# Retention's values as one block product of seven, and the second retention beside its output product, in a two-layer hybrid decoder

## The chip, the cores and the metric

The kernel runs on one core of a Trainium2 chip. The metric is the device time of one execution in microseconds (us); the time of a version is the median of several runs. All products use fp32 data that is split into a high and a low part in the fp32r format, so that three matmuls make one product of full precision.

## The reference, cut to what matters

The program is a decoder trunk of two layers over 512 tokens and a model width of 1024. Each layer computes, from the normalised input h:

```
z   = h @ W_in            # attn q,k,v | ret q,k,v,g | gate_a | gate_b
A   = sliding-window attention(q, k, v) with rotary q/k and sinks
B   = retention(ret q, ret k, ret v), normed per head, * silu(ret g)
y   = sigmoid(gate_a) * (A @ W_a) + sigmoid(gate_b) * (B @ W_b)
x   = x + y @ W_out
x   = x + relu(RMSNorm(x) @ W_up)^2 @ W_down
```

Retention has 4 heads with keys of 128 and values of 256 columns. Its values are the product of the normalised input (512 x 1024) with a 1024 x 1024 part of W_in. That product is what the change computes in another way.

## The kernel before, in words

**Data.** Activations lie transposed in SBUF: a tile `xh`/`xl` of 8 k-tiles of 128 features x 512 tokens (high and low part of the input times the norm's gain). The norm's factor per token is applied where a product is evacuated from PSUM. `products` (L350 to L357) issues three matmuls for each pair of operands: high by high (L355), low of one by high of the other (L356, L357). There are two pools of PSUM banks of 128 x 512: `ps_mm` with five and `ps_aux` with three.

**Weights.** All weights come in units of 128 x 1024 (512 KB). `unit_order` (from L56) lists them in the order in which TensorE uses them. SyncE loads a unit into one of five `raw` buffers (L192), four units ahead (`AHEAD`); ACT makes its high part (`hi<-raw`, L308), VectorE the low part (`lo<-raw,hi`, L309), three units ahead (`SPLIT`), into four buffers each. The load of a unit waits until the buffer's last unit has been split.

**Sums of weights.** The MLP's products already use a block scheme with seven block products in place of eight. It needs sums of weight blocks, which GpSimd makes in DRAM: `sum_steps` (L205 to L234) yields steps of one copy and one accumulate (DMA with an addition), each 512 KB or 1 MB. `pace` (L238 to L246) is called behind many evacuations; at every second call a one-column copy on GpSimd (`mark`) waits for that evacuation, and then the next step's DMAs are issued. A copy is accumulated on one step later, and the accumulate waits for it.

**Order of a layer's first half.** The q/k/v group and the chunks of q; then eight chunks of gate_a, with the attention as `background`: a generator, of which `advance` runs one piece at certain points of the chunks, and `drain` the rest. Then `qk(0)` (retention's key and query of head 0), four chunks of retention's gate (`rg0` to `rg3`), `drain`, `qk(1)`, `load_decay(0)`, `values(0)`, the product with w_a, `qk(2)` and `qk(3)` with `retention(0)` as background, `values(1)`, `drain`, `retention(1)` as background beside `rg4` to `rg7` and four chunks of gate_b, `drain`, the product with w_b, w_out, and the MLP. The scheduler of the framework puts each engine's instructions in its final order. The engines run their own lists in order and meet at semaphores.

**The lines of this case.**

- `values(pair)` (L826 to L845): for two heads, 4 units of weights. The input blocks are the stationary operand; the weights move. Four banks, one for each block of 128 tokens, 96 matmuls of 128 x 512. Evacuation by ACT (L378) and VectorE (L379) with the norm's factor as a column scale.
- `weighted(n)` (L722 to L725): the attention's output of a block of 128 tokens: two banks `pv`, per bank a copy on ACT (`whole<-pv`, L724) and an addition on VectorE (L725), then `split` (L375, L376), which writes `a_h` and `a_l`; in the profile these rows are `r<-whole`. They are the input of the product with w_a.
- `rotate` (L594 to L601): two half copies on ACT (`rot<-mm`, L595, L596) and three operations on VectorE, for each key and query.
- `silu(i)` (L865, L866): the sigmoid of retention's gate (`sig<-z`) and its product.
- `load_decay` (L941 to L943): loads the decay matrices of two heads into a buffer of `big` (`dm`), 512 KB.
- the product with w_a: four units, eight chunks of 12 matmuls. Each ends with `mixed[c] = mixed[c] * ps` on VectorE (L1001, `x<-x,mm`) and a `pace`.
- `beside` and `put_k`/`put_q`: rotated q and k, then copies of 64 KB inside SBUF on SyncE's queue (`r<-qlo`, `r<-r`), which place the two heads of a group beside each other for the scores.
- `Head` (L880 on): `scores` (`ret`, with the decay applied by VectorE at L895), `outputs` (`r`), `norm`, `finish`, which writes `ret[2h]` and `ret[2h+1]`, the input of w_b.
- `group` (L414 on): a product of four banks over four units, with an optional call between units.

`big` has six buffers of 128 x 1024 in turn, for tables, decay, `z`, sums and the like.

Of the kernel before, what the change touches and what calls it, by code (L numbers as in the profile page):

```python
# [40 lines left out]
O_GA = O_RG + RET_HEADS * RET_V  # L41
O_GB = O_GA + D

N_IN = 46
N_BLOCK = 8
N_PAIR = 14
UNIT = 1024
# [8 lines left out]
def unit_order(layer):  # L56

    order = [("w_in", i) for i in range(4 + 2 + 8 + 2 + 4 + 2)]
    order += [("w_in", i) for i in range(22, 26)]
    order += [("w_a", i) for i in range(4)]  # L60
    order += [("w_in", i) for i in range(26, 42)]
    order += [("w_b", i) for i in range(4)]
    order += [("w_in", i) for i in range(42, 46)]
# [48 lines left out]


@with_exitstack
def decoder(ctx, tc, xT, x_first, w_in, w_a, w_b, w_out, w_up, w_pair, w_down, w_end, tables, decay, band, g_last, out):
    nc = tc.nc
    weights = {"w_in": w_in, "w_a": w_a, "w_b": w_b, "w_out": w_out, "w_up": w_up, "w_down": w_down}

# [60 lines left out]
    def load_until(n):  # L179
        while state["loaded"] < min(n, len(order)):  # L180
            i = state["loaded"]
            layer, name, j = order[i][:3]
            if name == "pair":
                load_part(i)
            elif name == "block":
                load_block(i)
            else:
                raws[i] = raw_tile()
                for at in halves(i):
                    queue = nc.scalar if i == 0 and at.start == 0 else nc.sync  # L190
                    source = w_end[j] if name == "w_end" else weights[name][layer, j]
                    queue.dma_start(raws[i][:, at], source[:, at])  # L192
                    if i < 3:
                        load_x()
            state["loaded"] += 1
# [6 lines left out]
    sums_up = [dram.tile([N_PAIR, P, UNIT], F32, name=f"sums_up{l}") for l in range(DEPTH)]  # L202
    sums_down = [dram.tile([N_BLOCK, P, 2 * UNIT], F32, name=f"sums_down{l}") for l in range(DEPTH)]
    sums_last = dram.tile([P, 2, UNIT], F32, name="sums_last")

    def sum_steps(layer):

        whole = N_BLOCK if layer < DEPTH - 1 else N_BLOCK - 1
        jobs = []
        for e in range(N_BLOCK):  # L210
            if e:
                jobs += [(sums_up[layer][n], w_pair[layer, n], UNIT) for n in (2 * e - 2, 2 * e - 1)]
            if e < whole:
                jobs.append((sums_down[layer][e], w_down[layer, e], 2 * UNIT))
        last = None
        for job in jobs + [None]:
            if job:
                to, source, n = job
                nc.gpsimd.dma_start(to, source[:, :n])
            if last:  # L220
                to, source, n = last
                nc.gpsimd.dma_start(to, source[:, n // 2 : n // 2 + n], accum_op=ALU.add)
# [63 lines left out]
    def add_block(i):  # L286
        e, part = order[i][2:]
        if part in (2, 4) and e < N_BLOCK - 1:
            raws[i] = raws.pop(i - 2)
            nc.vector.tensor_tensor(raws[i], raws[i], raws.pop(i - 1), ALU.add)  # L290

    def split_until(n):
        while state["split"] < min(n, len(order)):
            i = state["split"]
            load_until(i + AHEAD)
            name, part = order[i][1], order[i][-1]
            if name == "pair":
                add_part(i)
            elif name == "block":
# [4 lines left out]
            for at in (LEFT,) if name == "pair" and part == 3 else halves(i):  # L304
# [2 lines left out]
                else:  # L307
                    nc.scalar.activation(hi[:, at], raw[:, at], AF.Copy)  # L308
                nc.vector.tensor_tensor(lo[:, at], raw[:, at], f32(hi[:, at]), ALU.subtract)  # L309
            if not (name == "pair" and part < 2 or name == "block" and part < 4 and order[i][2] < N_BLOCK - 1):  # L310
                raws.pop(i)
            parts[i] = (hi, lo)
            state["split"] += 1
# [101 lines left out]
    def group(name, layer, moving, evacuates, meanwhile=None, low_last=None):  # L415
# [3 lines left out]
        for u in range(4):  # L419
# [6 lines left out]
            if low_last:  # L426
# [151 lines left out]
    def layer_body(layer):  # L578
# [48 lines left out]

        def put_k(ps):
            r = rotate(ps, attn_tabs, layer == 0)
            lo = big("klo")[:, 0, :]  # L630
            for g in range(N_KV):
                nc.scalar.activation(kh[g], r, AF.Copy)
# [27 lines left out]
        def put_q(c):  # L660
            def put(ps):
                r = rotate(ps, attn_tabs, layer == 0 and c < 2)
                if c % 2 == 0:
                    qlo[:] = [big("qlo")]
                lo = qlo[0][:, c % 2, :]
# [158 lines left out]

        rv = {}

        def values(pair):

            banks = [bank(ps_mm, "rv") for _ in range(NB)]
            for u in range(4):  # L830
                hi, lo = unit("w_in", layer)
                for j in range(2):
                    k = 2 * u + j
                    cols = slice(j * T, (j + 1) * T)
                    for b, ps in enumerate(banks):
                        at = slice(b * P, (b + 1) * P)
                        products(
                            ps, [((xh[:, k, at], xl[:, k, at]), (hi[:, cols], lo[:, cols]))], k == 0, k == KD - 1
                        )
                    advance()  # L840
            for b, ps in enumerate(banks):
                hi, lo = slots.one(), slots.one()
                split(view(hi), view(lo), ps, rms_mix.columns[:, b : b + 1])
                rv[pair, b] = (hi, lo)
                pace(f32(view(hi)))  # L845

        rg, rg_next = {}, {}

# [142 lines left out]
        for u in range(4):  # L991
            hi, lo = unit("w_a", layer)
            for j in range(2):
# [5 lines left out]
                    pairs.append(((hi[:, cols], lo[:, cols]), aT[k]))  # L999
                products(ps, pairs, True, True)  # L1000
                nc.vector.tensor_tensor(mixed[c], mixed[c], ps, ALU.mult)  # L1001
                pace(mixed[c])
# [12 lines left out]

# [13 lines left out]
        def put_mixed(c):  # L1029
            def put(ps):  # L1030
                m = temp("m")
                nc.vector.tensor_tensor(m, ps, gates[c], ALU.mult)
                nc.vector.tensor_tensor(m, m, mixed[c], ALU.add)
                hi, lo = slots.one(), slots.one()
                split(view(hi), view(lo), m)
                ms[c] = (hi, lo)

            return put

        rT = [tuple(view(s) for s in ret[k]) for k in range(KD)]  # L1040
        group("w_b", layer, rT, [put_mixed(c) for c in range(4)])
        for c in range(4, KD):
            gate_tile(c)
            chunk("w_in", layer, xs, gate(gates[c]))
# [3 lines left out]
            slots.give(*ret.pop(k))  # L1048


        source = xT if layer == 0 else spill
        for c in range(KD):
            nc.sync.dma_start(x[:, c, :], source[:, c, :])

        def put_x(c):
            def put(ps):
                nc.vector.tensor_tensor(x[:, c, :], x[:, c, :], ps, ALU.add)
                scaled_input(c, g_mlp)
                squared_input(c, g_mlp)

            return put
# [452 lines left out]
def _w_in_units(w):  # L1514
# [17 lines left out]
    units += qk(0)  # L1532
    units += _units_chunks(w, O_RG + r(T))
    units += qk(1)
    units += _units_group(w, O_RV + r(T))
    units += qk(2) + qk(3)
    units += _units_group(w, O_RV + T + r(T))
    units += _units_chunks(w, O_RG + T + r(T))
    units += _units_chunks(w, O_GB + r(D))
    return units  # L1540
# [2 lines left out]
def _pairs(w):  # L1543
# [2 lines left out]
    return [  # L1546
        np.concatenate([a[:, :H], b[:, :H], b[:, H:], a[:, H:]], 1) for a, b in zip(units[::2], units[1::2])
    ]


def _down_blocks(w):
# [42 lines left out]
def _laid_out(x, g_mix, w_in, sinks, w_a, w_b, w_out, g_mlp, w_up, w_down, g_final):  # L1594
# [9 lines left out]
        "xT": xT,  # L1604
        "x_first": np.concatenate([sinks, gains, xT[:, 0, :]], 1),
        "w_in": _stack(w_in, _w_in_units),
        "w_a": _stack(w_a, lambda w: _units_chunks(w[wa_rows], r(D))),
        "w_b": _stack(w_b, _half_grouped),
        "w_out": _stack(w_out, _half_grouped),
# [27 lines left out]
```

## Time and profile before

| | us |
|---|---|
| median of 3 runs | 1478.72 |
| runs | 1478.6, 1478.72, 1480.43 |
| the profiled execution's own time | 1480.34 |
| its span in the profile | 1478.6 |
| TensorE busy | 1467.4 |
| VectorE busy | 1079.6 |
| ACT busy | 914.0 |
| GpSimd busy | 195.3 |

The profile is of one execution. Its own time is 1.7 us above its span, and 1.6 above the median of the runs. PE is TensorE, DVE is VectorE, SP is SyncE (its queue of DMA issues is SPq). A row of a timeline has the start, the duration, the engine, the line, the operation, and output and input by the program's names; in brackets stands the idle time before it and what ended it. A matmul's duration in the profile is modelled and overlaps the next one's: the spacing of starts is what a matmul costs. A row of the DMA view has the number of issues, the size of each and the median time from issue to landing.

### The profile page before, as it was taken

The numbers are of one execution on the slowest core, as the hardware profiler recorded it, in microseconds if no ns is written. First come the engines' busy times: TensorE is split into PE (matmuls) and PEld (weight loads), VectorE is DVE, ScalarE is ACT, GpSimd is POOL, SyncE is SP. The second block draws the span as 40 slices with busy tenths as digits, with TensorE's granted clock in tenths as the row PEclk, the third lists the DMA queues.
The fourth block names the chain that finished last, engine by engine and source line by source line (L and its number), as shares of the span: only waits on it lengthen the run. The fifth ranks groups of instructions, "written<-read, shape, count | busy, mean of one in ns | idle before, by whom it ended". The sixth has DMA issues, their size and how long they took to land.

```text
span 1478.6 us, 21314 instructions
## 1 busy us (share of the span) xinstructions
PE 1467.4 (99%) x7799; PEld 1266.5 (86%) x7799; DVE 1079.6 (73%) x1639; ACT 914.0 (62%) x1501; POOL 195.3 (13%) x282
## 2 busy tenths in 40 slices
PE   9999999999999999999999999999999999999998
PEld 7888888888889999999888888888888899999997
DVE  6878568664577888888778686686546778888885
ACT  6656445533467777777756573555325777777775
POOL 0101121001001111112201012111000111111120
PEclk9999999999999999999999999999999999999999
DMA  7663996767315677666956539976432377777664
GB/s 259 174 191 82 310 271 162 197 184 214 118 65 192 188 197 190 167 184 183 302 172 207 157 101 309 267 190 184 146 128 89 114 202 195 189 197 186 174 191 148
DMA packets 92984, 272.61 MB, mean 184 GB/s; under 512 B 10832, under 2 KB 10960, under 8 KB 89040
## 3 DMA queue, kind: packets, MB, share of 16 engines
q1 hardware_dynamic: 60816, 169.27, 32.9%
q0 software_dynamic: 31344, 100.68, 30.9%
q8 instruction: 61, 1.00, 0.3%
q10 hardware_dynamic: 720, 1.31, 0.2%
q14 instruction: 43, 0.35, 0.1%
HBM read 231.37 MB, written 99.09 MB: 223 GB/s over the span
## 4 chain that ended last, share of the span: by engine, by line
PE 98%; DMA 1%; ACT 1%; DVE 0%; issue 0%; ACTq 0%
PE mm L355 25%; PE mm L356 25%; PE mm L357 25%; PE b L355 3%; PE b L356 3%; PE b L357 3%; PE rv L355 2%; PE rv L357 2%; PE rv L356 2%; PE mm L370 1%; PE score L737 1%; PE pT L702 1%; PE r L356 1%; PE r L357 1%; PE r L355 1%; DMA y<-eu 1%
## 5 line engine op out<-in xcount | busy, mean ns | idle before, releaser
L308 ACT ACTIVATE hi<-raw 128x1024 fp32r<-128x1024 f32 (+1 forms) x363 | 369.6, 1019 | 331.1 <-PE mm L356 225.2
L309 DVE TENSOR_TENSOR lo<-raw,hi 128x1024 fp32r<-128x1024 f32 (+1 forms) x364 | 423.7, 1170 | 163.5 <-ACT hi L308 162.3
L355 PE MATMUL mm<-xh,hi 128*128 128x512 f32 (+1 forms) x976 | 345.2, 356 | 1.8 <-DVE z L856 1.0
L356 PE MATMUL mm<-xl,hi 128*128 128x512 f32 (+1 forms) x976 | 344.2, 355 | 0.0
L357 PE MATMUL mm<-xh,lo 128*128 128x512 f32 (+1 forms) x976 | 341.9, 355 | 0.0
L355 PE MATMUL mm<-r,hi 128*128 128x256 f32 (+1 forms) x736 | 238.8, 324 | 0.5 <-ACT mm L1184 0.5
L357 PE MATMUL mm<-r,lo 128*128 128x256 f32 (+1 forms) x736 | 238.9, 325 | 0.0
L356 PE MATMUL mm<-r,hi 128*128 128x256 f32 (+1 forms) x736 | 238.8, 324 | 0.0
L355 PEld LDWEIGHTS mm<-xh,hi 128*128 128x128 f32 x976 | 185.2, 190 | 26.8 <-ACT xh L378 1.5
L356 PEld LDWEIGHTS mm<-xl,hi 128*128 128x128 f32 x976 | 185.3, 190 | 24.3
L357 PEld LDWEIGHTS mm<-xh,lo 128*128 128x128 f32 x976 | 184.2, 190 | 24.2
L355 PEld LDWEIGHTS mm<-r,hi 128*128 128x128 f32 x736 | 139.8, 190 | 13.7 <-ACT mm L1184 0.7
L356 PEld LDWEIGHTS mm<-r,hi 128*128 128x128 f32 x736 | 139.8, 190 | 13.0
L357 PEld LDWEIGHTS mm<-r,lo 128*128 128x128 f32 x736 | 139.8, 190 | 11.4
L1326 POOL DMA_DIRECT2D y<-eu x56 | 62.3, 1353 | 370.0 <-DVE eu L1311 370.0
L356 PE MATMUL mm<-lo,r 128*128 128x512 f32 (+1 forms) x276 | 104.3, 387 | 0.0
L357 PE MATMUL mm<-hi,r 128*128 128x512 f32 (+1 forms) x276 | 101.3, 386 | 0.0
L355 PE MATMUL mm<-hi,r 128*128 128x512 f32 (+1 forms) x276 | 98.5, 390 | 0.4 <-ACT r L375 0.2
L1326 POOL DMA_DIRECT2D y<-y x56 | 55.8, 1010 | 112.2 <-ACT y L1321 106.5
L355 PE MATMUL b<-hi,r 128*128 128x512 f32 x180 | 70.4, 391 | 0.0
L356 PE MATMUL b<-lo,r 128*128 128x512 f32 x180 | 70.2, 390 | 0.0
L357 PE MATMUL b<-hi,r 128*128 128x512 f32 x180 | 67.8, 389 | 0.0
(271 smaller groups left out, 2335.6 us busy)
## 6 DMA issues: line engine op xcount, KB each, us to landing
raw<-w_in_in SPq DMA_DIRECT2D x89, 512.0 KB, 5.6
sums_down<-w_down_in POOLq DMA_DIRECT2D x30, 1024.0 KB, 11.1
sums_up<-w_pair_in POOLq DMA_DIRECT2D x56, 512.0 KB, 9.9
raw<-w_down_in SPq DMA_DIRECT2D x45, 512.0 KB, 7.0
raw<-w_pair_in SPq DMA_DIRECT2D x84, 256.0 KB, 3.6
y<-y POOLq DMA_DIRECT2D x64, 256.0 KB, 9.0
y<-eu POOLq DMA_DIRECT2D x62, 256.0 KB, 7.8
raw<-sums_down SPq DMA_DIRECT2D x30, 512.0 KB, 7.1
```

The source lines that it names most:

```text
L308: nc.scalar.activation(hi[:, at], raw[:, at], AF.Copy)
L309: nc.vector.tensor_tensor(lo[:, at], raw[:, at], f32(hi[:, at]), ALU.subtract)
L355: nc.tensor.matmul(ps, ah, bh, start=start and i == 0, stop=False, **more)
L356: nc.tensor.matmul(ps, ah, bl, start=False, stop=False, **more)
L357: latest[0] = nc.tensor.matmul(ps, al, bh, start=False, stop=stop and i == n - 1, **more).ins
L370: latest[0] = nc.tensor.matmul(ps, w[:, cols(j, c)], moving[k][low], start=first, stop=bool(final)).ins
L702: nc.tensor.transpose(pt[:, i * P : (i + 1) * P], sm[:, at : at + P], ident)
L737: nc.tensor.matmul(ps[:, g * w : (g + 1) * w], q_s[g][:, c, at], part[:, keys], start=i == 0, stop=i == 1)
L1326: nc.gpsimd.dma_start(y[:, 2 * j + m, i * T : (i + 1) * T], t, **how)
```

## The change

Both halves of retention's values become one product. The input is cut into quarters (2 halves of the features x 2 halves of the tokens), the weights into four blocks of 512 x 512, and seven block products with sums of blocks replace eight. Weights move, as before; the stationary operand is a quarter of the input or a sum of quarters ("forms").

- The weights' blocks lie in a new tensor `w_rv` in DRAM. Two of its sums per unit are made by GpSimd's steps (`sums_rv`: per layer two copies and two accumulates of 1 MB, put at the head of the list of jobs), two more by VectorE from units in SBUF (`add_values`). The units of a layer become 14 (7 block products x 2), 10 of them loaded.
- The forms of the input are made by `Turned`: SyncE loads the layer's input again (`xg<-xT` in the first layer, `xg<-spill` in the second, 4 x 512 KB), ACT scales it by the norm's gain (four times 128 x 512 per pair of tiles), VectorE makes differences and ACT and VectorE split them. `load(0)` stands before `qk(1)` in the program, `build(0)` and `load(2)` behind it, `build(2)` in the product with w_a.
- The product with w_a now follows `qk(1)` directly; the values come behind it. `load_decay(0)` moves behind `build(2)`.
- `values` holds six banks in three pairs and adds block products into them; a bank of `ps_aux` is opened by one matmul of the input with `ones`. It copies one pair into another, and keeps two pairs in SBUF (`kept`).
- `retention(0)` starts inside `values`, before its last block product; `qk(2)`, `qk(3)`, `rg4` and `rg5` run beside it at a rate of 1.2 pieces a call. `retention(1)` starts before `rg6`, and its rest is drained behind the second unit of w_b's group (`second_pair`), whose third and fourth unit use its outputs; `group` calls `advance` once per k-tile.
- `pace` calls are added for keys, queries, the mix and w_out's evacuations, and go from the values and the product with w_a.

By the instruction lists of the two programs, TensorE has 7739 matmuls instead of 7785 (46 fewer, all of 128 x 512), VectorE 58 and ACT 52 instructions more.

```diff
-    order += [("w_in", i) for i in range(22, 26)]
     order += [("w_a", i) for i in range(4)]
-    order += [("w_in", i) for i in range(26, 42)]
+    order += [("rv", part, u) for part in range(7) for u in range(2)]
+    order += [("w_in", i) for i in range(22, 34)]
...
+        jobs = [(sums_rv[layer][u], w_rv[layer, u], 2 * UNIT) for u in range(2)]
...
+    def add_values(i):
+        part = order[i][2]
+        if part in (2, 4):
+            raws[i] = raws.pop(i - 2)
+            nc.vector.tensor_tensor(raws[i], raws[i], raws.pop(i - 4), ALU.add)
...
+            for j in range(0 if low_last else 2):
+                advance()
...
+            def load(self, ks):
+                self.b = [big("xg") for _ in range(2)]
+                for part, b in enumerate(self.b):
+                    k = ks + 4 * part
+                    nc.sync.dma_start(b, source[:, k : k + 2, :])
...
+            def build(self, ks):
+                for part, b in enumerate(self.b):
+                    for i in range(2):
+                        col = g_mix * KD + ks + 4 * part + i
+                        nc.scalar.activation(b[:, i, :], b[:, i, :], AF.Copy, scale=gain[:, col : col + 1])
+                (b11, b12), (b21, b22) = ((b[:, :, :H], b[:, :, H:]) for b in self.b)
+                two = temp("t2").rearrange("p (a t) -> p a t", t=H)
+                nc.vector.tensor_tensor(b22, b22, b12, ALU.subtract)
+                nc.vector.scalar_tensor_tensor(two, b11, -1.0, b22, ALU.mult, ALU.subtract)
+                nc.vector.tensor_tensor(b11, b11, b12, ALU.subtract)
+                nc.vector.scalar_tensor_tensor(b21, two, -1.0, b21, ALU.mult, ALU.subtract)
+                hi, lo = self.halves(ks, 0)
+                split(hi[:, 0:2, :], lo[:, 0:2, :], b11)
+                split(hi[:, 2:4, :], lo[:, 2:4, :], two)
...
+                split(hi, lo, self.b[1].rearrange("p a (b t) -> p b a t", t=H))
...
+            a, c = ([bank(ps_mm, "rv") for _ in range(2)] for _ in range(2))
+            b = [bank(pool, "rv") for pool in (ps_mm, ps_aux)]
+            nc.tensor.matmul(b[1], ones, xh[:, 0, :], start=True, stop=True)
...
+            multiply(a, quarter(0, 0))
+            for m in range(2):
+                nc.scalar.activation(b[m], a[m], AF.Copy)
+            multiply(c, turned[1])
+            five = keep(1, c, -1)
+            multiply(b, turned[2], False)
+            turned.free(0)
+            two = keep(1, b, 1)
+            multiply(a, quarter(1, 0), False)
+            put(0, 0, a, 1)
+            multiply(c, quarter(1, 1), False)
+            put(0, 1, c, 1, two)
+            multiply(b, turned[3], False)
+            put(1, 1, b, -1, five)
+            while_last()
+            multiply(b, turned[4], False, advance)
+            turned.free(1)
+            put(1, 0, b, -1)
...
+        source = xT if layer == 0 else spill
+        turned = Turned()
+        turned.load(0)
         qk(1)
-        load_decay(0)
-
-        values(0)
+        turned.build(0)
+        turned.load(2)
...
+            if u == 1:
+                turned.build(2)
+                load_decay(0)
...
-        background.append(retention(0))
-        qk(2)
-        qk(3)
-        values(1)
+        values(turned, lambda: background.append(retention(0)))
+        qk(2, 1.2)
+        qk(3, 1.2)
+        for i in (4, 5):
+            chunk("w_in", layer, xs, put_rg(i), 1.2)
         drain()
         background.append(retention(1))
-        for i in range(4, 8):
+        for i in (6, 7):
             chunk("w_in", layer, xs, put_rg(i))
...
-        drain()
...
-        rT = [tuple(view(s) for s in ret[k]) for k in range(KD)]
-        group("w_b", layer, rT, [put_mixed(c) for c in range(4)])
+        rT = []
+
+        def second_pair():
+            drain()
+            rT.extend(tuple(view(s) for s in ret[k]) for k in range(4, KD))
+
+        rT.extend(tuple(view(s) for s in ret[k]) for k in range(4))
+        group("w_b", layer, rT, [put_mixed(c) for c in range(4)], {1: second_pair})
```

More of the change, by code (lines that the diff above doesn't have):

```diff
@@ L42 @@
 O_GB = O_GA + D
-N_IN = 46
+N_IN = 38
 N_BLOCK = 8
@@ L114, in decoder @@
 @with_exitstack
-def decoder(ctx, tc, xT, x_first, w_in, w_a, w_b, w_out, w_up, w_pair, w_down, w_end, tables, decay, band, g_last, out):
+def decoder(ctx, tc, xT, x_first, w_in, w_rv, w_a, w_b, w_out, w_up, w_pair, w_down, w_end, tables, decay, band, g_last, out):
     nc = tc.nc
@@ L290, in add_block, with load_values @@
             nc.vector.tensor_tensor(raws[i], raws[i], raws.pop(i - 1), ALU.add)
+    def load_values(i):
+        layer, _, part, u = order[i]
+        if part in (2, 4):
+            return
+        raws[i] = raw = raw_tile()
+        source, at = {
+            0: (w_rv, 0),
+            1: (sums_rv, 1),
+            3: (w_rv, 3),
+            5: (sums_rv, 0),
+            6: (w_rv, 2),
+        }[part]
+        source = source[layer][u] if part in (1, 5) else source[layer, u]
+        nc.sync.dma_start(raw, source[:, at * UNIT : (at + 1) * UNIT])
+    def add_values(i):
+        part = order[i][2]
+        if part in (2, 4):
+            raws[i] = raws.pop(i - 2)
+            nc.vector.tensor_tensor(raws[i], raws[i], raws.pop(i - 4), ALU.add)
     def split_until(n):
@@ L294, in split_until @@
             i = state["split"]
+            name, part = order[i][1], order[i][-1]
+            if name == "rv":
+                add_values(i)
             load_until(i + AHEAD)
-            name, part = order[i][1], order[i][-1]
             if name == "pair":
@@ L309, in split_until @@
                 nc.vector.tensor_tensor(lo[:, at], raw[:, at], f32(hi[:, at]), ALU.subtract)
-            if not (name == "pair" and part < 2 or name == "block" and part < 4 and order[i][2] < N_BLOCK - 1):
+            kept = {
+                "pair": part < 2,
+                "block": name == "block" and part < 4 and order[i][2] < N_BLOCK - 1,
+                "rv": name == "rv" and order[i][2] < 4,
+            }
+            if not kept.get(name):
                 raws.pop(i)
@@ L825, in layer_body, with __init__, halves, free @@
         rv = {}
[L827 to L845, printed above, removed]
+        class Turned:
+            def __init__(self):
+                self.groups = [[slots.four() for _ in range(2)] for _ in range(2)]
+                self.parts = {}
+            def load(self, ks):
[3 more added lines that the diff above has]
+                    nc.sync.dma_start(b, source[:, k : k + 2, :])
+            def halves(self, ks, which):
+                t = self.groups[which][ks // 2][0]
+                return [t[:, 2 * i : 2 * i + 2, :].rearrange("p a (b t) -> p (a b) t", t=H) for i in range(2)]
+            def build(self, ks):
[12 more added lines that the diff above has]
+                split(hi[:, 2:4, :], lo[:, 2:4, :], two)
+                for i in range(2):
+                    for n in range(2):
+                        self.parts[1 + n, ks + i] = tuple(t[:, 2 * n + i, :] for t in (hi, lo))
+                hi, lo = (t.rearrange("p (b a) t -> p b a t", a=2) for t in self.halves(ks, 1))
+                split(hi, lo, self.b[1].rearrange("p a (b t) -> p b a t", t=H))
+                for i in range(2):
+                    for n in range(2):
+                        self.parts[4 - n, ks + i] = tuple(t[:, n, i, :] for t in (hi, lo))
+            def free(self, which):
+                for _, own in self.groups[which]:
+                    slots.give(*own)
+            def __getitem__(self, n):
+                return [self.parts[n, k] for k in range(4)]
@@ L1048, in layer_body @@
             slots.give(*ret.pop(k))
-        source = xT if layer == 0 else spill
         for c in range(KD):
@@ L1548, in _pairs, with _value_blocks @@
     ]
+def _value_blocks(w):
+    w, blocks = w[:, O_RV : O_RV + D], []
+    for u in range(2):
+        parts = []
+        for f, k in ((0, 0), (T, 0), (T, T), (0, T)):
+            rows = w[k + 2 * u * P : k + 2 * (u + 1) * P, f : f + T]
+            parts.append(rows.reshape(2, P, T).transpose(1, 0, 2).reshape(P, UNIT))
+        blocks.append(np.concatenate(parts, 1))
+    return blocks
 def _down_blocks(w):
```

51 lines of the change are left out of this document (46 added, 5 removed).

## The prediction, made before the changed kernel ran

> **What bounds the kernel now.** I read the page first: the busy shares, the slices of the span and the chain that ended last.
>
> ```profile
> PE 1467.4 (99%) x7799; PEld 1266.5 (86%) x7799; DVE 1079.6 (73%) x1639; ACT 914.0 (62%) x1501; POOL 195.3 (13%) x282
> ...
> PEclk9999999999999999999999999999999999999999
> DMA  7663996767315677666956539976432377777664
> ...
> PE 98%; DMA 1%; ACT 1%; DVE 0%; issue 0%; ACTq 0%
> ```
>
> TensorE is busy 99% of the span at full clock and is 98% of the chain, so the time is the number of matmuls times their spacing, plus the few places where TensorE waits. A removed matmul pays only if nothing it covered becomes late. Next I read the timeline of PE for what one matmul costs, where the values of the first layer begin, and the groups by shape for how many there are.
>
> ```profile
> 148.78 0.39 PE L723 MATMUL pv<-r,r 128*128 128x512 f32 x1
> ...
> 149.91 0.39 PE L355 MATMUL rv<-hi,xh 128*128 128x512 f32 x1
> ...
> 152.63 0.39 PE L355 MATMUL rv<-hi,xh 128*128 128x512 f32 x1
> ```
>
> ```profile
> L355 PE MATMUL rv<-hi,xh 128*128 128x512 f32 x128 | 49.5, 390 | 0.0
> ```
>
> The 390 ns of a row overlap with the next matmul and are not the price. Twelve matmuls lie between the starts 149.91 and 152.63, so one costs 0.2267 us.
>
> **What the change removes.** The values take 3 x 128 = 384 matmuls. The product of seven needs 336 (per layer 7 blocks x 2 units x 2 banks x 2 k-tiles x 3), and each layer adds one matmul that only opens a bank: 46 fewer, all 128x512. 46 x 0.2267 = **-10.4 us**, counted from the instruction lists, so "it doesn't save matmuls" is no rival. The added splits, sums and scalings on ACT and VectorE (52 and 58 instructions) cost nothing by themselves as long as TensorE's products run meanwhile; the copies and accumulates for the sums of weights have the same cover, except where named below.
>
> **What moves: w_a loses its cover.** Before, the product with w_a followed values(0), 96 matmuls (22 us) after the attention ended. Its input is the attention's output, and the last piece of that (`r<-whole`, L375) was made in ACT's queue while the values ran. In the changed program, w_a comes straight after the attention's last `pv`, with one bank-opening matmul and six `ret` matmuls (three 128x512, three 128x384) between. On ACT, `r<-whole` stands behind: two copies of `pv`, two sigmoids, two rotation copies, and, new, two scalings of the reloaded input (`xg`, 128x512 each), the first of which waits for a load. ACT's timeline of the second layer shows the same queue without the new part:
>
> ```profile
> 884.24 1.27 ACT L724 ACTIVATE whole<-pv 64x512 f32<-64x512 f32 x2 [3.47 <-PE pv L723]
> 885.53 1.15 ACT L865 ACTIVATE sig<-z 128x512 f32<-128x512 f32 x2
> 886.71 0.60 ACT L595 ACTIVATE rot<-mm 64x512 f32<-64x512 f32 x1
> 887.32 0.59 ACT L596 ACTIVATE rot<-mm 64x512 f32<-64x512 f32 x1
> 887.93 0.63 ACT L375 ACTIVATE r<-whole 128x512 fp32r<-128x512 f32 x1
> ```
>
> From the PE timeline of that layer:
>
> ```profile
> 879.73 0.39 PE L355 MATMUL rv<-hi,xh 128*128 128x512 f32 x1
> ...
> 883.13 0.39 PE L356 MATMUL rv<-lo,xh 128*128 128x512 f32 x1
> ...
> 884.49 0.39 PE L723 MATMUL pv<-r,r 128*128 128x512 f32 x1
> ```
>
> The last `pv` starts at 884.49; `whole` is done at 885.51, 1.0 later. Fourteen value matmuls (879.73 to 883.13) ran ahead of it that no longer do, so in the same clock of the trace the new last `pv` starts at 884.49 - 14 x 0.227 = 881.3. In the first layer four matmuls that followed the last `pv` now precede it: 148.78 + 4 x 0.227 = 149.7. The seven matmuls after it last 0.23 + 3 x 0.23 + 3 x 0.17 = 1.4 (384 columns by proportion), so w_a could start at 151.3 and 883.0. ACT's queue needs from the last `pv` 1.0 + 1.15 + 1.2 + 1.15 (two scalings at the sigmoids' price) + 0.63 = 5.15 us: not before 154.85 and 886.45. That is **3.5 us** per layer in which TensorE has nothing else, even if the reload is there.
>
> **Is the reload there?** In the instruction lists SyncE issues the first `xg` directly behind the load that follows one particular split (`lo<-raw,hi`, the second to last before the last `pv`). That split's place is a row of VectorE or of SyncE's own queue in before: issues at 141.75 and 878.14, so `xg` goes out at about 142.1 and 878.5.
>
> ```profile
> 141.75 0.33 SPq L192 DMA_DIRECT2D raw<-w_a_in  x1
> ...
> 146.02 0.33 SPq L192 DMA_DIRECT2D raw<-w_a_in  x1
> 146.40 0.98 SPq L943 DMA_DIRECT2D dm<-decay_in  x2
> ```
>
> ```profile
> 878.14 0.33 SPq L192 DMA_DIRECT2D raw<-w_a_in  x1
> 882.05 0.33 SPq L192 DMA_DIRECT2D raw<-w_in_in  x1
> 882.43 1.03 SPq L943 DMA_DIRECT2D dm<-decay_in  x2
> ```
>
> Their landings, from the DMA view of windows around each issue (first layer, then second):
>
> ```profile
> raw<-w_a_in SPq DMA_DIRECT2D x1, 512.0 KB, 9.7
> ...
> raw<-w_a_in SPq DMA_DIRECT2D x1, 512.0 KB, 8.4
> dm<-decay_in SPq DMA_DIRECT2D x1, 512.0 KB, 13.1
> ```
>
> ```profile
> raw<-w_a_in SPq DMA_DIRECT2D x1, 512.0 KB, 10.2
> ...
> raw<-w_in_in SPq DMA_DIRECT2D x1, 512.0 KB, 9.5
> dm<-decay_in SPq DMA_DIRECT2D x1, 512.0 KB, 12.8
> ```
>
> ```profile
> raw<-w_in_in SPq DMA_DIRECT2D x89, 512.0 KB, 5.6
> ```
>
> The last row is the page's median for a weight load, 5.6. The loads above, of the same size, landed in order at 151.4, 154.4, 159.5 and 888.3, 891.5, 895.2: one every 3 to 5 us. Each took 8 to 13, because GpSimd's copies of weight sums were moving too, as they will be (the same marks, behind the same `late` and `z` instructions, release 2.5 MB of them there).
>
> ```profile
> 877.22 0.87 POOL L222 DMA_DIRECT2D sums_down<-w_down_in  x1
> ...
> 883.81 0.53 POOL L219 DMA_DIRECT2D sums_down<-w_down_in  x1 [0.28 <-issue]
> ```
>
> `xg` is as large and is second in that queue, so I take the second landing: 154.4 and 891.5. Then two scalings and the split, 1.78 us: w_a starts at 156.2 and 893.3, **4.9 and 10.3 us** late instead of 3.5 and 3.5. Bounds: 3.5 each (landed by 153 and 884.7), and the third landing, 10.0 and 14.0. [...]
>
> **Clock.** What a gap of 5 or 10 us in mid-kernel does to TensorE isn't shown by before: its costliest group of matmuls has 1.8 us of idle time in all. The nearest rows are the kernel's first products:
>
> ```profile
> L355 PE MATMUL mm<-xh,hi 128*128 128x512 f32 (+1 forms) x976 | 345.2, 356 | 1.8 <-DVE z L856 1.0
> ```
>
> ```profile
> 5.64 2.08 PE L355 MATMUL mm<-xh,hi 128*128 128x512 f32 x4 [0.79 <-ACT xh L378]
> ...
> 10.47 0.40 PE L355 MATMUL mm<-xh,hi 128*128 128x512 f32 x1
> ```
>
> Twelve matmuls take 4.83 us where 2.72 are due: 2.1 us too much. Bounds 0 to 2.1 per gap; I take 2.1 after the long one and 1.0 after the shorter, **3.1**. [...]
>
> **The second pair of reloads, and the banks.** `xg` tiles 3 and 4 reuse buffers: the last is issued only after the first build's splits, ten VectorE instructions after the second tile is scaled, and `x<-x,mm`, which frees the banks that the values need, stands behind the next forms in VectorE's queue.
>
> ```profile
> 178.53 0.69 DVE L1001 TENSOR_TENSOR x<-x,mm 128x512 f32<-128x512 f32 x1 [2.08 <-PE mm L357]
> ```
>
> ```profile
> L309 DVE TENSOR_TENSOR lo<-raw,hi 128x1024 fp32r<-128x1024 f32 (+1 forms) x364 | 423.7, 1170 | 163.5 <-ACT hi L308 162.3
> ```
>
> First layer: second tile at 159.5, scaled by 160.65, ten instructions at 0.69: 167.55, load 5.6: 173.15, scaled by 174.3, seven more and one wide split (1.2): 180.3. The second bank of the values is due 102 matmuls after w_a's start, at 179.3: 1.0 late. Second layer: 895.2, and by the same steps 916.0 against 916.4: nothing. With 9.7 us for the load, 5.1 and 3.7. I take **1.0**.
>
> **Attention's start.** GpSimd now copies 4 MB per layer earlier, beside the 64 KB copies of q and k that the first scores need. The DMA view of the first stage (20 to 80 us) and of the second layer's (740 to 830):
>
> ```profile
> r<-qlo SPq DMA_DIRECT2D x16, 64.0 KB, 2.2
> ```
>
> ```profile
> r<-qlo SPq DMA_DIRECT2D x16, 64.0 KB, 3.6
> ```
>
> The second has more of GpSimd's transfers beside it and is 1.4 slower. I take half of that in each layer, **1.4** in all; bounds 0 and, by 1.4 and as much again per layer, 5.6.
>
> **The second retention** moves beside the first half of w_b's product: it needs its outputs only at the third weight unit; the products in between (48 matmuls, 10.9 us) cover the norm and the two finishes, some ten ACT and VectorE instructions at 0.6 to 0.7. I take 0. Without that cover it costs these 6 to 7 us a layer; a gain is excluded, since TensorE had no idle time there.
>
> **The sum**, against the profiled execution's own 1480.34: -10.4 + 4.9 + 10.3 + 3.1 + 1.0 + 1.4 = **+10.3**, 1490.6. The median of the runs is 1.6 lower, 1478.7: **1489** us. The measurement tells about 0.2% (3 us) from no change.
>
> **Rivals.**
> - *Reload in time, small terms present.* Before, loads in a quiet stretch land in 5.6, and if `xg` does too, both waits are the 3.5 of ACT's queue: -10.4 + 7.0 + 1.0 + 1.4 = -1.0, 1477.7: no change. Against: the crowded landings above.
> - *Faster.* One mechanism: the wait at w_a is no longer than ACT's queue (`xg` landed before 884.7 and 153), and the banks and copies hide: -10.4 + 7.0 = -3.4, 1475.3. It decides from waits below 10.4 in all: with the first layer's 4.9 and no slow clock, when `xg` of the second layer lands before 886.7. A wait of nothing would give 1468.3, but ACT's order holds the scalings ahead of `r<-whole`.
> - *Slower still.* `xg` lands where the third load did (159.5 and 895.2): 5.1 + 3.7 more, and with late banks (3.7 to 7.8) besides: +19 to +27, 1498 to 1506.
>
> **Chances.** Forecast, +5 to +16 (1484 to 1495): 0.53. Reload in time: 0.15. Faster: 0.17. Slower still: 0.15. So faster 0.17, same 0.15, slower 0.68. The range leaves out a third of the third case and most of the fourth, under 0.2 in all: 1473 to 1499.
>
> **What would show it.** Right: PE idle for 4 to 11 us just before the first w_a matmul in each layer, released by ACT's `r<-whole` (which itself waited for `xg`'s scaling and that for the DMA); slower matmuls just after; 336 + 2 `rv` matmuls at 0.227 spacing with no idle between. Wrong: ACT scales `xg` without a wait; PE idle under 4 us there; or idle time instead at the first scores, between w_a and the values, or ahead of w_b's third unit.

## The result, and the profile after

The changed kernel took 1506.18 us (median of four runs, 1502.61 to 1507.71) against 1479.53 before, a ratio of 1.0178 with a 95% interval of 1.0165 to 1.0191. It is 1.8% slower, where +0.7% was forecast, and it lies above the forecast's range. The execution with the profile took 1502.61, the fastest of the four; what follows is read from it, against the 1480.34 of before's profiled execution: +22.3. The medians are 26.7 apart; what the other three executions lost beyond the profiled one, 4.4 us in the median, stands in no trace.

The page of the changed kernel, busy times, granted clock and the chain that ended last:

```profile
PE 1465.7 (98%) x7753; PEld 1262.4 (84%) x7753; DVE 1124.4 (75%) x1697; ACT 949.0 (63%) x1553; POOL 218.1 (15%) x294
...
PEclk9999999999999999999999998999999999999999
...
PE 91%; DMA 4%; DVE 2%; ACT 2%; issue 1%; SPq 0%; ACTq 0%; DVEq 0%
```

Busy time of PE went down by only 1.7 us (a matmul of 512 columns counts 0.63 us at a granted clock of 0.50, 0.39 at 1.00). In the chain, PE's share fell from 98% to 91%, and DMA, VectorE and ACT now end waits that are on the path. By line, the chain's DMA share is named `r<-qlo` (2%) and `xg<-spill` (1%). That says where to look, not what was lost: in the kernel of experiment 8, which is faster than before, PE's share of the chain is 93%.

I took each start of a matmul in PE's timeline, subtracted the spacing that its width costs undisturbed (0.2268 us for 512 columns, 0.173, 0.1145 and 0.10 for 384, 256 and 128), and summed what is left, the idle and slow time, by stage:

| stage | before | after | difference |
|---|---|---|---|
| 0 to 20 us, start of the kernel | 4.9 | 2.6 | -2.2 |
| first layer, the attention's start (40 to 80) | 0.6 | 9.4 | +8.8 |
| first layer, from the attention's end to the first w_a matmuls (140 to 180) | 0.2 | 7.9 | +7.7 |
| second layer, the attention's start (780 to 820) | 0.7 | 4.9 | +4.3 |
| second layer, late in the attention (860 to 880) | 1.5 | 4.4 | +2.9 |
| second layer, w_a (880 to 920) | 0.0 | 10.9 | +10.9 |
| everything else | 24.5 | 24.6 | +0.1 |

Together +32.5; with -10.4 for 46 matmuls that is +22.1 of the 22.3. In the values themselves and in the stages of both retentions there is nothing to find: the groups of the new product by shape have no idle time before them.

```profile
L386 PE MATMUL rv<-hi,r 128*128 128x512 f32 x64 | 24.9, 389 | 0.0
...
L386 PE MATMUL rv<-hi,xh 128*128 128x512 f32 x48 | 18.7, 389 | 0.0
```

(64 + 48) x 3 is 336, as counted.

**The attention's start.** PE's timeline of the changed kernel:

```profile
68.05 0.41 PE L771 MATMUL score<-r,r 128*128 128x128 f32 x2 [0.86 <-DMA r<-qlo]
75.26 0.66 PE L771 MATMUL score<-r,r 128*128 128x128 f32 x2 [5.14 <-DMA r<-qlo]
```

TensorE stands 5.14 us for one of the 64 KB copies of q. The same copies in the DMA view, first the stage from 20 to 80 us, then 740 to 830:

```profile
r<-qlo SPq DMA_DIRECT2D x16, 64.0 KB, 11.1
...
r<-qlo SPq DMA_DIRECT2D x16, 64.0 KB, 9.0
```

The medians were 2.2 and 3.6 before; the slowest now takes 14.2. The queues' shares between 50 and 60 us, before and then after, show what else was in flight:

```profile
q1 hardware_dynamic: 520, 0.82, 32.3%
q0 software_dynamic: 80, 0.66, 21.5%
```

```profile
q0 software_dynamic: 341, 2.53, 86.3%
q1 hardware_dynamic: 403, 0.56, 16.1%
```

And the first step of GpSimd's in each kernel:

```profile
54.51 1.63 POOL L243 COPY mark<-x 128x1 f32<-128x1 f32 x1 [51.85 <-DVE x L798]
```

```profile
41.40 0.49 POOL L246 COPY mark<-rot 128x1 f32<-128x1 f32 x1 [38.74 <-DVE rot L633]
```

q0 is GpSimd's queue: the 2.62 MB that it moved from 20 to 80 us before are the bytes of GpSimd's three issues there. With the new `pace` calls behind keys and queries its steps begin at 41 us instead of 54, four of them within 17 us, and take 86% of the DMA engines' time just when SyncE's small copies are wanted.

**The wait at w_a**, first and then second layer, PE and ACT:

```profile
160.27 0.50 PE L386 MATMUL ret<-late 128*128 128x512 f32 x1 [1.93 <-DVE whole L759]
...
163.51 2.08 PE L386 MATMUL mm<-r,hi 128*128 128x512 f32 x4 [1.30 <-ACT r L406]
165.38 0.63 PE L387 MATMUL mm<-r,hi 128*128 128x512 f32 x1
```

```profile
900.39 0.50 PE L386 MATMUL ret<-late 128*128 128x512 f32 x1 [1.93 <-DVE whole L759]
...
908.22 2.07 PE L386 MATMUL mm<-r,hi 128*128 128x512 f32 x4 [6.30 <-ACT r L406]
```

```profile
901.11 0.59 ACT L628 ACTIVATE rot<-mm 64x512 f32<-64x512 f32 x1
906.31 1.33 ACT L882 ACTIVATE xg<-xg,x 128x512 f32<-128x512 f32 x2 [4.61 <-DMA xg<-spill]
907.55 0.61 ACT L406 ACTIVATE r<-whole 128x512 fp32r<-128x512 f32 x1
```

The issues of the reload, second and then first layer, and the landing in the first:

```profile
893.24 1.38 SPq L872 DMA_DIRECT2D xg<-spill  x2
...
154.92 0.90 SPq L872 DMA_DIRECT2D xg<-xT_in  x2
...
xg<-xT_in SPq DMA_DIRECT2D x2, 512.0 KB, 5.2
```

In the second layer this is what the prediction describes: ACT stands 4.61 us at the reload, `r<-whole` behind it, and PE 6.30 behind that. The reload was issued at 893.24 and its first tile landed 13.1 us later. In the first layer it was issued at 154.92 and took 5.2 in the median of its two tiles: ACT scaled it without a wait, and what is left (3.7 us in two pieces) is ACT's queue, the forecast's minimum of 3.5. Part of the wait shows at `ret` (1.93 us), whose PSUM bank comes free with `whole` on VectorE. The rest of the first layer's 7.9 is slow clock and a wait of 0.97 us at 143.75 for `z`.

**The clock.** Windows of the changed kernel: the waiting, the first w_a matmuls, and after (the columns are the window, busy times, the granted clock, the DMA share and GB/s).

```profile
157.00:163.40 6.40, 3.28 (x12) 1.95 (x11) 6.10 (x9) 5.57 (x10) 1.54 (x3) 0.83 1.00 381
163.40:168.00 4.60, 4.49 (x11) 3.53 (x12) 4.53 (x9) 3.70 (x7) 1.33 (x3) 0.50 1.01 192
168.00:172.00 4.00, 4.00 (x19) 3.30 (x18) 3.57 (x6) 1.47 (x4) 0.73 (x1) 1.00 0.94 292
```

After both waits TensorE ran at half its clock: 0.50, matmuls 0.43 us apart, for some 4 us. That costs 2.2 us in the first layer and 2.0 in the second. But the clock had fallen before the last of these waits. Stretches ahead of the fall and behind it, first and then second layer:

```profile
157.00:161.10 4.10, 2.17 (x10) 1.35 (x9) 3.83 (x6) 3.29 (x7) 1.54 (x3) 1.00 0.98 381
161.20:163.40 2.20, 1.01 (x4) 0.50 (x2) 2.17 (x4) 2.17 (x4) 0.00 (x0) 0.50 1.05 385
...
896.00:902.00 6.00, 3.98 (x17) 2.65 (x15) 4.61 (x7) 4.69 (x7) 1.53 (x3) 0.99 1.02 262
902.00:908.00 6.00, 0.00 (x0) 0.00 (x0) 1.68 (x3) 1.69 (x3) 0.00 (x0) 0.50 1.05 337
```

In the first layer the granted clock fell at about 161.2, ahead of the 1.30 us wait; in the second at about 902, when the wait of 6.30 us had only begun. What stood before the fall in both is the 1.93 us wait at `ret`. The slow clock is part of the attention's start too: 0.50 from 72.5 to 79.2 and from 809.7 to 813.1.

### The profile page after: what moved, and what is told of

Same layout as the page of the kernel before. It is cut to its first block, busy times and chain, and to the rows that moved or that the text cites. A ratio compares the mean times of both kernels' runs of the same rounds, so it can differ in the third digit from the quotient of the medians.

```text
span 1500.8 us, 21396 instructions
## 1 busy us (share of the span) xinstructions
PE 1465.7 (98%) x7753; PEld 1262.4 (84%) x7753; DVE 1124.4 (75%) x1697; ACT 949.0 (63%) x1553; POOL 218.1 (15%) x294
## 4 chain that ended last, share of the span: by engine, by line
PE 91%; DMA 4%; DVE 2%; ACT 2%; issue 1%; SPq 0%; ACTq 0%; DVEq 0%
PE mm L386 24%; PE mm L387 24%; PE mm L388 24%; PE b L386 3%; PE b L387 3%; PE b L388 3%; DMA r<-qlo 2%; PE rv L386 2%; PE rv L388 2%; PE rv L387 2%; PE mm L401 1%; DMA xg<-spill 1%; PE score L771 1%; DVE lo L335 1%; PE r L388 1%; PE r L387 1%
## 5 line engine op out<-in xcount | busy, mean ns | idle before, releaser
L334 ACT ACTIVATE hi<-raw 128x1024 fp32r<-128x1024 f32 (+1 forms) x375 | 382.4, 1020 | 319.3 <-PE mm L387 190.0
L335 DVE TENSOR_TENSOR lo<-raw,hi 128x1024 fp32r<-128x1024 f32 (+1 forms) x376 | 438.8, 1173 | 145.5 <-ACT hi L334 143.6
L386 PEld LDWEIGHTS mm<-xh,hi 128*128 128x128 f32 x976 | 185.4, 190 | 26.7 <-ACT xh L409 1.2
L387 PEld LDWEIGHTS mm<-xl,hi 128*128 128x128 f32 x976 | 185.5, 190 | 24.5
L388 PEld LDWEIGHTS mm<-xh,lo 128*128 128x128 f32 x976 | 184.6, 190 | 24.6
L270 DVE TENSOR_TENSOR raw<-raw 128x512 f32<-128x512 f32 x56 | 38.6, 690 | 36.5 <-DMA raw<-w_pair_in 25.4
```

Of the source, the lines that this page charges most:

```text
L270: nc.vector.tensor_tensor(raws[i][:, at], last[:, LEFT], last[:, RIGHT], ALU.add)
L386: nc.tensor.matmul(ps, ah, bh, start=start and i == 0, stop=False, **more)
L387: nc.tensor.matmul(ps, ah, bl, start=False, stop=False, **more)
L388: latest[0] = nc.tensor.matmul(ps, al, bh, start=False, stop=stop and i == n - 1, **more).ins
```

## The experiments

The theory after the result: the slowdown is the early weight sums beside the copies of q and k, plus a product with w_a that has lost its cover; the product of seven itself is worth its matmuls. Rivals were other causes of the late attention, ACT's order against the reload's landing as the cause at w_a, and the second retention. The kernel before, in the same comparisons, took 1480.0 in the first four and 1479.0 in the last four.

**1. Late sums.** The `pace` calls behind keys and queries go; five gate chunks of a layer call it twice. The same steps, the same bytes, later.

```diff
             r = rotate(ps, attn_tabs, layer == 0)
-            pace(r)
...
                 r = rotate(ps, attn_tabs, layer == 0 and c < 2)
-                pace(r)
...
                 pace(mixed[c])
+                if c >= 3:
+                    pace(mixed[c])
```

> The changed kernel (1506.2) without its pace calls behind keys and queries; five of the eight gate chunks of a layer call pace twice instead, from the fourth on, so that GpSimd makes the sums of weights, the values' among them, after the copies of q and k that the first scores need. Theory: GpSimd's early transfers delay those copies, and TensorE's idle time at the attention's start (8.4 us more than before in the first layer, 4.4 and 2.9 in the second) goes: 1490 to 1494, and the 64 KB copies land in 2 to 4 us again instead of 8 to 14. Rival: the attention starts late for another reason (VectorE's or SyncE's order): 1504 to 1508.

Measured: 1484.26 us, 21.9 less than the changed kernel (ratio to before 1.0032, 1.0020 to 1.0044). That is more of a fall than expected. The copies of q, 20 to 80 us and then 740 to 830:

```profile
r<-qlo SPq DMA_DIRECT2D x16, 64.0 KB, 2.4
...
r<-qlo SPq DMA_DIRECT2D x16, 64.0 KB, 2.2
```

The idle and slow time at the attention's start is 0.6 us in the first layer and 2.0 in the second, and the stage before the first layer's w_a profits as well: 3.2 us in place of 7.9, most of it one wait of 2.33 behind ACT, at full clock (1.00 from 140 to 180). So moving GpSimd's steps gained about 22 us; the theory's place was right, its price too low. Why the first layer's w_a gains isn't separated: the attention is on time, GpSimd's transfers lie elsewhere there too, and on ACT `r<-whole` now stands ahead of the scalings:

```profile
151.04 0.63 ACT L406 ACTIVATE r<-whole 128x512 fp32r<-128x512 f32 x1
151.58 2.55 ACT L882 ACTIVATE xg<-xg,x 128x512 f32<-128x512 f32 x4
```

What stays is the second layer: 9.8 us around w_a, and 4.5 in its attention from 850 to 862.

**2. `r<-whole` ahead of the scalings on ACT.**

```diff
-                split(a_h[:, :, at], a_l[:, :, at], whole.rearrange(
+                last_split[:] = split(a_h[:, :, at], a_l[:, :, at], whole.rearrange(
...
-        turned.build(0)
+        with tc.issue_after(last_split[0]):
+            turned.build(0)
```

> The changed kernel with the first build held behind the split of the attention's last block, so that on ACT r<-whole stands ahead of the scalings of the reloaded input; nothing else moves. Rival, which the prediction's text suggests: the queue order on ACT makes the wait at w_a; w_a then starts 2.4 us late per layer instead of 4.7 and 10.9, and the time falls by about 11, to 1495. Theory: the reload itself is the bound. Its second pair is issued only after the first build's splits, and the values' banks come free behind the second build, so that the wait moves from ahead of w_a to ahead of the values: a fall of 0 to 3, 1503 to 1506.

Measured: 1500.85 us, 5.3 less: between the two. The wait at w_a of the second layer fell from 6.30 to 0.49, but part came back where the theory put it, at the values:

```profile
906.36 1.05 PE L386 MATMUL mm<-r,hi 128*128 128x512 f32 x2 [0.49 <-ACT r L406]
```

```profile
938.44 0.50 PE L386 MATMUL rv<-hi,r 128*128 128x512 f32 x1 [1.41 <-DVE x L1131]
```

In the first layer the wait fell from 1.30 to 0.49, but the stage kept 7.7 of its 7.9 us: behind the 1.93 us at `ret` the clock fell all the same, and TensorE worked at 0.50 for 6.7 us.

```profile
162.50:169.20 6.70, 6.37 (x14) 4.63 (x15) 6.51 (x11) 5.22 (x10) 1.95 (x3) 0.50 0.98 254
```

Idle and slow time in the second layer from 880 to 940 is 7.0 us instead of 10.9; in the profiled executions the attention's start was slower here (9.0 from 800 to 820 instead of 4.8), which hides some of the gain.

**3. The kernel before, with early `pace` calls only.** The two lines that experiment 1 took out are put into the kernel before.

> The kernel before (1479.5) with the two pace calls that the change adds behind keys and queries, and nothing else: GpSimd's steps start beside the 64 KB copies of q and k. Theory: these transfers alone delay the attention: 6 to 13 us slower, 1486 to 1492, with idle time of TensorE that DMA r<-qlo ends at 55 to 77. Rival: only the new 4 MB of the values' sums are too many, or another part of the change is the cause: within 2 us, 1478 to 1482.

Measured: 1499.92 us, 19.9 slower (ratio 1.0131, 1.0114 to 1.0148), more than the 6 to 13 expected. Nothing of the values, the forms or w_a is in this kernel. PE's timeline and the copies (20 to 80 us):

```profile
70.89 0.41 PE L739 MATMUL score<-r,r 128*128 128x128 f32 x2 [3.73 <-DMA r<-qlo]
72.93 0.69 PE L739 MATMUL score<-r,r 128*128 128x128 f32 x2 [1.64 <-DMA r<-qlo]
```

```profile
r<-qlo SPq DMA_DIRECT2D x16, 64.0 KB, 8.2
```

By stage, idle and slow time is 11.3 us from 40 to 80 (0.6 before), 4.7 from 780 to 820 (0.7) and 6.5 from 820 to 920 (2.1), and unchanged at 0.2 from 140 to 180, where the values still follow the attention. The two lines alone cost about as much as moving them away gains. The rival, that only the values' own 4 MB are too much, is out: here GpSimd moves what it always moved, only sooner.

**4. The first reload issued before retention's gate chunks.**

```diff
         qk(0, PACE)
+        source = xT if layer == 0 else spill
+        first_xg = load_xg(0)
...
-        turned.load(0)
+        turned.b = first_xg
         qk(1)
```

> The changed kernel with the first pair of the input's reload issued before the retention gate's chunks (behind qk of head 0) instead of before qk of head 1; the rest as it is. Theory: the reload's landing sets the wait at w_a and, in chain, the second pair; with the tiles there in time, w_a waits 2 to 3.5 us per layer instead of 4.7 and 10.9, and the values don't wait: a fall of 8 to 11, 1495 to 1498. Rival: ACT's queue or the second pair's chain holds the values in any case: a fall of 0 to 3.

Measured: 1500.39 us, 5.8 less, below the theory's 8 to 11. In the second layer the wait of PE for `r<-whole` is gone (6.30 to under 0.3), and the values wait for nothing: 4.3 us from 880 to 920 instead of 10.9. The 1.93 at `ret` stays, and 2.0 of slow clock behind it, without any longer wait. The gain is in the second layer, since the first layer's reload had not been late (7.1 us before its w_a instead of 7.9). The late landing makes the second layer's wait.

**5. The second retention beside w_b, alone,** put into the kernel before: `advance` in `group`, no `drain` ahead of it, `second_pair` behind the second unit, as in the change. The second retention still starts before `rg4` here, and not before `rg6`, so it has two chunks more to run beside.

> The kernel before (1480.0) with only the second part of the change: the second retention runs on beside the gate_b chunks and the first half of w_b's product, and is drained behind its second unit; the values, their order and GpSimd's steps are those of before. Prediction's claim: this costs and gains nothing, 1478 to 1482. Rival: the norm's chain is late at w_b's third unit: 1483 to 1490, with idle time of TensorE there.

Measured: 1480.42 us, ratio 1.0006 (0.9997 to 1.0015). Nothing lost, nothing gained.

**6. Late sums, early load and `r<-whole` first,** that is 1, 2 and 4 together.

> The kernel with late sums (1484.3) and, with it, the input's first reload issued before the retention gate's chunks and r<-whole ahead of the scalings on ACT. Theory: of its waits at w_a (3.1 us in the first layer, 9.8 with what stands around it in the second) 2 to 4 per layer stay, which is ACT's queue behind the last pv: 1476 to 1480. Rival: the second reload's chain takes the place of the first: 1482 to 1485.

Measured: 1482.19 us (1.0023, 1.0013 to 1.0033): the rival's range and 2.1 less than experiment 1, whose ratio (1.0020 to 1.0044) overlaps this one, so that a gain over it isn't shown. The second layer's w_a now waits 1.93 and 0.49, but the values wait 1.57 and 1.15 for `x<-x,mm`, VectorE's evacuations, which stand behind the second build. Here a wait taken from the first reload went in part to the second; in experiment 4, where the first build isn't held behind the split, the values didn't wait.

**7. Late sums, with `qk` of head 2 between the attention's end and w_a** as cover (48 matmuls).

```diff
+    order += [("w_in", i) for i in (22, 23)]
     order += [("w_a", i) for i in range(4)]
...
         qk(1)
+        qk(2)
         turned.build(0)
...
-        values(turned, lambda: background.append(retention(0)))
-        qk(2, 1.2)
-        qk(3, 1.2)
-        for i in (4, 5):
-            chunk("w_in", layer, xs, put_rg(i), 1.2)
+        values(turned, lambda: None)
+        background.append(retention(0))
+        qk(3, 2.0)
+        for i in (4, 5, 6):
+            chunk("w_in", layer, xs, put_rg(i), 1.2)
```

> The kernel with late sums, with qk of head 2 (48 matmuls, 10.9 us) moved from behind the values to ahead of the product with w_a, as cover for the attention's end; the first retention then starts behind the values. Theory: what makes w_a wait is missing cover, so its waits go but for what the late reload (at 154 and 891 in the old kernel's clock) leaves behind it on ACT, some 2 us per layer: 1473 to 1478. Rival: the waits move to the values or to the retention: 1482 to 1486.

Measured: 1480.26 us (1.0009, 0.9998 to 1.0020), 4.0 less than experiment 1 and between the two expectations. No wait is left at w_a in either layer; as the rival says, they went to the values. In the second layer the reload is still late, and its second pair with it: ACT waits 9.76 us for the last tile, and the values 3.30 behind VectorE.

```profile
919.40 1.33 ACT L883 ACTIVATE xg<-xg,x 128x512 f32<-128x512 f32 x2 [9.76 <-DMA xg<-spill]
```

```profile
922.20 0.47 PE L387 MATMUL rv<-hi,r 128*128 128x512 f32 x1 [3.30 <-DVE x L1132]
```

**8. The same with the early load.**

> The same with the input's first reload issued before the retention gate's chunks as well. Theory: nothing waits at w_a or at the values, so that nearly all of the 46 matmuls (10.4 us) is gained over the kernel before, less 1 to 4 us of idle time at the attention of the second layer: 1470 to 1474. Rival: no better than without the early load, 1475 to 1478.

Measured: 1472.88 us, the theory's range; ratio to before 0.9957 (0.9945 to 0.9969). This version beats both kernels, by 0.4% and 2.2%. The page:

```profile
PE 1457.5 (99%) x7753; PEld 1258.5 (86%) x7753; DVE 1123.3 (76%) x1697; ACT 952.4 (65%) x1557; POOL 206.1 (14%) x294
...
PEclk9999999999999999999999999999999999999999
...
PE 93%; DMA 3%; DVE 2%; ACT 1%; issue 0%; SPq 0%; ACTq 0%
```

PE's busy time is 9.9 us below that of before, and the granted clock is 1.00 from 20 to 1460. From 140 to 200 us and from 860 to 940 there are 0.8 and 1.3 us of idle or slow time; the largest wait left in these layers' first halves stands at the second layer's attention:

```profile
853.38 0.74 PE L770 MATMUL score<-r,r 128*128 128x256 f32 x4 [0.55 <-DVE st L778]
...
855.79 0.50 PE L755 MATMUL pv<-r,r 128*128 128x512 f32 x1 [1.68 <-ACT r L407]
```

## Why the prediction was wrong, point by point

- **Matmuls removed, -10.4.** Right: 336 + 2 `rv` matmuls at full spacing. Experiment 8 gets 8.3 of it in the profiled execution and 6.1 by the medians.
- **w_a without cover, 4.9 and 10.3.** Right in mechanism in the second layer, and nearly in size: 3.7 and 8.6. In the second layer the reload, second in the queue behind a crowded load, took 13.1 us as read from before's rows (13.0). In the first its first tile landed in 4.8 instead of 12.3: GpSimd's next transfer was issued only at 159.6, so the crowd that the forecast took from before's rows wasn't there, and ACT's queue alone decided. That isn't the late attention's doing, for in experiment 1, with the attention on time, the first tile took 4.8 as well. Experiments 2 and 4 tell the two causes apart: the late landing makes the second layer's wait, and ACT's order lets `r<-whole` stand behind it; either remedy alone takes the 6.30 away (0.49 and under 0.3 are left).
- **Clock, 3.1.** 4.2 was measured (2.2 and 2.0), the upper bound that the kernel's first products gave. The size is near in part by luck. No run shows that the 2.1 us of those products are slow clock, and the forecast tied the term to the gaps of 5 and 10 us at w_a: the clock fell to 0.50 behind the 1.93 us at `ret` (at 161.2 and 901.9), and in experiment 4 the second layer pays 2.0 without the long wait. The length of a wait alone doesn't decide: behind 2.33 us in experiment 1 (149.4 to 151.7) the clock stayed at 1.00 and the next four matmuls took 1.20 us, behind 2.31 us in experiment 6 (149.1 to 151.4) it was 0.50 until 154.5 and they took 2.08. What does decide is not shown.
- **Second reloads and banks, 1.0.** Nothing in the changed kernel; but the chain is real: experiments 2, 6 and 7 met it in the second layer when w_a's wait was shorter.
- **Attention's start, 1.4 in all, bounds 0 to 5.6.** This is the step that failed, in its size. It measured 8.8 + 4.3 = 13.1 us, and late in the second layer's attention 2.9 more. Of the 12.0 us between the forecast's +10.3 and the profiled +22.3, this term alone makes 11.7; the other misses nearly cancel. The prediction's own signs of being wrong name "idle time instead at the first scores", and there it was, beside the wait at w_a. The mechanism was named, GpSimd's copies beside the 64 KB copies of q and k; the price was half of the difference between two stages of before (2.2 and 3.6 us to land), and in both of those only one to three of GpSimd's transfers were issued while the copies were. The two new `pace` calls put four steps into 17 us, q0's share rose from 21.5% to 86.3%, and the copies took 11.1 and 9.0 us. Experiment 3 puts the two lines at +19.9 in a kernel without the rest of the change, experiment 1 at -21.9 in the changed one.
- **Second retention, 0.** Right (experiment 5).
- **The rivals.** "Slower still" named 1498 to 1506 but for another reason, a later reload. That reason didn't hold, so that 1506.18 stands beside its upper end by luck.
- **Not foreseen:** the start of the kernel, 2.2 us quicker in the profiled execution of after; the idle and slow time of the first 20 us is 2.5 to 5.1 us in the ten profiled executions, one of each kernel.

What stays open: the 2 to 3 us at the second layer's attention (852 to 856 in experiment 8), which 1.5 us of before's table stand against. It is there with late sums and without any wait at w_a. That the values' matmuls no longer run between the attention's last blocks doesn't explain it as it stands: before, the first of them started 4.8 us ahead of the last `pv` (879.73 and 884.49), and this wait ends 24 us ahead of it (855.79 and 880.20). What it comes from is not shown.

## What to carry to other kernels

A transfer that nobody waits for can be the dearest part of a change (19.9 us in experiment 3): ask what else is in flight at its new moment, and price small copies that something waits for by the share of the DMA engines that the newcomers take, not by the landings of a quieter stage (here 86.3%, and 11.1 us instead of 2.2). When a stage is moved, its inputs lose the cover that the order gave them, and each wait that is removed alone shows the next in line; here only cover, early load and late sums together brought most of what the saved matmuls are worth, 6.1 of 10.4 us.

## What the runs showed that was not expected

Sixteen copies of 64 KB on SyncE's queue went from 2.2 to 11.1 us in the median when GpSimd's queue took 86.3% of the DMA engines' time, while q1 still moved 0.56 MB in those 10 us. And TensorE's granted clock fell to 0.50 behind a single wait of 1.93 us, in both layers; in experiment 2 it then stayed there for 6.7 us, of which TensorE was busy 6.37.
